# Rotary embedding on one core: one load merged, one store split in two, one small ScalarE copy moved back

## The chip, the cores and the metric

The kernel runs on 1 core of one Trainium2 chip. The metric is the time of one execution on the device in microseconds (us), so less is better. Before the change the median of 3 runs is 161.59 us; the three are 161.46, 161.59 and 163.9.

## The reference

The input `x` is 16 x 512 x 1024 float32 (33.55 MB), read as 16 heads of 64 numbers per token. Each head is cut into two halves of 32 and rotated by a table of cosines and sines that depends on the position alone:

```python
x = x.reshape(batch, seq, num_heads, head_dim)
x1, x2 = x[..., :half_dim], x[..., half_dim:]
rotated = np.concatenate([x1 * cos - x2 * sin,
                          x1 * sin + x2 * cos], axis=-1)
return rotated.astype(np.float32)
```

`cos` and `sin` are 512 x 32 float32. The output has the size of the input, so at least 67.1 MB cross between the chip's main memory (HBM) and the core's own memory.

## The kernel before

**Slabs and places.** `x` is cut into 8 slabs of 2 batches (4.19 MB each), which are worked on in pairs 0-1, 2-3, 4-5, 6-7. In a pair every one of the 128 partitions holds 16 successive tokens, 8 of the one slab and 8 of the other, so that a partition's 64 KB of a pair are contiguous in HBM, and one slab's share of it is 32 KB. There are three places in the core's memory, of a pair each. Slabs 0-5 fill them; slabs 6 and 7 are loaded into the places of slabs 0 and 1, once these have been stored.

**Transfers.** All loads of `x` are issued on SyncE's queue, all stores on ScalarE's, the two small tables ahead of everything on ScalarE's. Slabs 0, 1, 6 and 7 are loaded one by one (`load`, line 65, 128 rows of 32 KB each). Slabs 2-3 are loaded by two DMAs, one for even and one for odd partitions (line 83: 64 rows of 64 KB each). Slabs 4-5 are loaded by one DMA (128 rows of 64 KB). Slabs 0 to 3 are stored one by one (`store`, line 69); slabs 4-5 by two DMAs, of even and of odd partitions (line 162); slabs 6-7, the last, by one DMA of 128 rows of 64 KB (`store(6, 2)`).

**Table.** GpSimd makes a 0/1/-1 matrix (`pick`) and rounds cos and sin to bf16; TensorE spreads them by 8 small matmuls to the layout of the slabs, into two accumulators. The first half of the table (`tabs[0]`, for even slabs) is copied out by VectorE (line 113), the second (`tabs[1]`, for odd slabs) by ScalarE (line 144).

**Work on a slab.** ScalarE casts the slab to bf16 into the lower half of the place (`cast`); VectorE multiplies it twice with the table and adds the two with halves exchanged; ScalarE copies the sum back to float32 over the place, and the store is issued behind that copy. Slab 0 is worked in two passes, slab 7 in three. The copies of ScalarE stand in program order (`tc.keep_in_program_order`), and a cast runs ahead of the copies back by two slabs' places in the list: the cast of slab 2 stands in front of the copy back of slab 1, and so on. Line 138 in the profile is the helper `copy` by which all of ScalarE's copies go.

The order of ScalarE around the change is: cast slab 0 (two halves), copy `tabs[1]`, cast slab 1, copy back slab 0 (two halves), store 0, cast slab 2, copy back slab 1, store 1.

Of the kernel before, what the change touches and what calls it, by code (L numbers as in the profile page):

```python
# [2 lines left out]

# [4 lines left out]


@with_exitstack  # L10
def kernel(
    ctx: ExitStack,
    tc: tile.TileContext,
    x: bass.AP,
    cos: bass.AP,
    sin: bass.AP,
    num_heads: int,
    out: bass.AP,
):
    nc = tc.nc  # L20
    P = nc.NUM_PARTITIONS

    batch, seq, dim = x.shape
    nh = num_heads
    hd = dim // nh
    half = hd // 2
    bf16 = mybir.dt.bfloat16
    f32 = mybir.dt.float32

    nb = 2  # L30
    nslabs = batch // nb
    rpp = nb * seq // P
    W = rpp * dim
    TP = seq // rpp
    TW = rpp * half

    out_flat = out.rearrange("b s h d -> b s (h d)")

    singles = ctx.enter_context(tc.tile_pool(name="singles", bufs=1))
    pairs = ctx.enter_context(tc.tile_pool(name="pairs", bufs=3))  # L40
    psum = ctx.enter_context(tc.tile_pool(
        name="psum", bufs=1, space=bass.MemoryType.PSUM))


    def view(t, offset, *dims):
        return dataclasses.replace(t, offset=t.offset + offset,
                                   ap=[t.ap[0], *[list(d) for d in dims]])

    places = [pairs.tile([P, 2 * W], f32, tag="pair", name="pair") for _ in range(3)]


    def here(s, n=1):
        return view(places[s // 2 % 3], s % 2 * W, (1, n * W))


    def there(t, s, n=1):
        return bass.AP(tensor=t.tensor, offset=t.offset + s // 2 * 2 * P * W + s % 2 * W,  # L60
                       ap=[[2 * W, P], [1, n * W]])


    def load(s, n=1):
        nc.sync.dma_start(out=here(s, n), in_=there(x, s, n))  # L65


    def store(s, n=1):
        nc.scalar.dma_start(out=there(out_flat, s, n), in_=here(s, n))  # L69


    load(0)


    cos_sb = singles.tile([TP, TW], f32, tag="cos_sb")
    sin_sb = singles.tile([TP, TW], f32, tag="sin_sb")
    for t, src in ((cos_sb, cos), (sin_sb, sin)):
        nc.scalar.dma_start(out=t, in_=bass.AP(
            tensor=src.tensor, offset=src.offset, ap=[[TW, TP], [1, TW]]))

    load(1)
    for p in range(2):
        nc.sync.dma_start(out=here(2, 2)[p::2], in_=there(x, 2, 2)[p::2])  # L83
    load(4, 2)


    pick = singles.tile([TP, 4 * P], bf16, tag="pick")
    nc.gpsimd.memset(pick, 0.0)  # L88
    for h in range(2):
        for g in range(2):  # L90
            part = view(pick, (2 * h + g) * P, (TP // 2, 2 * P // TP), (1, TP // 2))
            nc.gpsimd.affine_select(  # L92
                out=part, in_=part, compare_op=mybir.AluOpType.not_equal,
                fill=1.0 - 2.0 * g, base=-h, pattern=[[0, 2 * P // TP], [-2, TP // 2]],
                channel_multiplier=1)

    tab1 = singles.tile([TP, 2 * TW], bf16, tag="tab1")
    for i, t in enumerate((cos_sb, sin_sb)):
        nc.gpsimd.tensor_copy(out=view(tab1, i * TW, (1, TW)), in_=t)  # L99

    accs, tabs = [], []
    for h in range(2):
        acc = psum.tile([P, 2 * rpp * hd], f32, tag=f"acc{h}", name="acc")
        for i in range(2):
            for f in range(2):
                nc.tensor.matmul(  # L106
                    view(acc, i * rpp * hd + f * half, (hd, rpp), (1, half)),
                    view(pick, (2 * h + i * f) * P, (1, P)),
                    view(tab1, i * TW, (half, rpp), (1, half)),
                    start=True, stop=True)  # L110
        accs.append(acc)
        tabs.append(singles.tile([P, 2 * rpp * hd], bf16, tag=f"tab{h}", name="tab"))
    nc.vector.tensor_copy(out=tabs[0], in_=accs[0])  # L113

    passes = []
    for s in range(nslabs):
        r = 0  # L120
        for n in {0: (4, 4), nslabs - 1: (4, 2, 2)}.get(s, (rpp,)):
            passes.append((s, r, n))
            r += n


    def halves(u):
        s, r, n = u
        t = here(s).bitcast(bf16)
        return [view(t, (2 * r + i * n) * dim, (1, n * dim)) for i in range(2)]


    def cast(u):
        s, r, n = u
        copy(halves(u)[0], view(here(s), r * dim, (1, n * dim)))


    def copy(out, in_):
        tc.keep_in_program_order(nc.scalar.copy(out=out, in_=in_))  # L138


    ahead = list(passes)
    for _ in range(2):
        cast(ahead.pop(0))
    copy(tabs[1], accs[1])
    cast(ahead.pop(0))
    for i, u in enumerate(passes):
        s, r, n = u
        while ahead and len(passes) - len(ahead) < (i + 2 if s < nslabs - 2 else len(passes)):
            cast(ahead.pop(0))
        lo, up = halves(u)  # L150
        for t, a in ((up, 0), (lo, rpp * hd)):
            nc.vector.tensor_mul(  # L152
                out=t, in0=lo,
                in1=view(tabs[s % 2], a + r * hd, (hd, n), (0, nh), (1, hd)))
        nc.vector.tensor_add(  # L155
            out=up, in0=up, in1=view(lo, half, (hd, n * nh), (-half, 2), (1, half)))

        copy(view(here(s), r * dim, (1, n * dim)), up)
        if r + n == rpp:
            if s == 5:  # L160
                for p in range(2):
                    nc.scalar.dma_start(out=there(out_flat, 4, 2)[p::2], in_=here(4, 2)[p::2])  # L162
            elif s == 7:
                store(6, 2)
            elif s < 4:
                store(s)
            if s < 2:
                load(s + 6)


# [1 line left out]
_INS = ['x', 'cos', 'sin', 'num_heads']  # L172
_OUTS = [((16, 512, 16, 64), 'float32')]

_NUMBERS = {'num_heads': 16}


# [26 lines left out]
```

## Time and profile before

| | |
|---|---|
| median of the runs | 161.59 us |
| time of the profiled execution | 161.8 us |
| its span, first to last instruction | 160.0 us |
| busy: VectorE, ScalarE | 107.9 us (67%), 114.3 us (71%) |
| busy: TensorE, GpSimd | 2.0 us, 2.6 us |
| HBM read, written | 33.69 MB, 33.55 MB |
| cast or copy back of a whole slab on ScalarE | 7.02 us |
| one of VectorE's three steps on a whole slab | 4.42 us |
| copy of half a table: VectorE, ScalarE | 1.23 us, 1.00 us |

The profile is of one execution. The span leaves out 1.8 us of the execution's time (161.8 - 160.0) at its start and end. "ACT" is ScalarE, "DVE" VectorE, "POOL" GpSimd, "SP" SyncE; a "q" behind an engine's name stands for its issuing of DMAs, which is not counted as busy time. A DMA's "landing" is the moment when its semaphore says that all of it has arrived. The core has 16 DMA engines, on which the DMAs of both queues run. A DMA's rows (here of 32 or 64 KB) are the packets that the profile counts; in tables by stretches of time the DMA share counts a packet with its whole time in the stretch in which it begins, so that a short stretch can show a share over 1, and the share times the length of the stretch is the time per engine of the packets that began in it.

### The profile page before, as it was taken

To read this page: it belongs to the slowest core of one execution; us is meant where nothing else is said; L and a number is where in the kernel's file an instruction comes from. 1 tells how busy PE (TensorE), PEld (TensorE's weight loads), DVE (VectorE), ACT (ScalarE), POOL (GpSimd) and SP (SyncE) were. 2 spreads that over 40 slices of the span, in tenths; PEclk is the share of its full clock that TensorE was granted. 3 is DMA by queue.
4 is the path that set the end of the run, shared out by engine and by line. 5 is a ranking of instruction groups with operands and counts; after the bars stand their busy time and mean duration, and the time that the engine had idled before them with its cause. 6 is when DMAs were issued, how large, how long until landed. Compare 5 with 4: busy or idle time off the path is not lost.

```text
span 160.0 us, 167 instructions
## 1 busy us (share of the span) xinstructions
PE 2.0 (1%) x8; PEld 1.0 (1%) x8; DVE 107.9 (67%) x34; ACT 114.3 (71%) x24; POOL 2.6 (2%) x11
## 2 busy tenths in 40 slices
PE   0001300000000000000000000000000000000000
PEld 0000100000000000000000000000000000000000
DVE  0000499999951999799889979998999998000000
ACT  3006959993089989998998999999879999500000
POOL 4000000000000000000000000000000000000000
DMA  7999999699599999999999999999997999989966
GB/s 262 401 401 410 426 491 524 262 524 524 254 401 410 606 426 393 393 393 393 467 451 393 434 483 393 401 500 410 393 590 328 524 393 393 524 360 426 524 262 262
DMA packets 1920, 67.24 MB, mean 420 GB/s; under 512 B 256, under 2 KB 384, under 8 KB 384
## 3 DMA queue, kind: packets, MB, share of 16 engines
q1 hardware_dynamic: 880, 33.55, 49.5%
q10 hardware_dynamic: 1040, 33.69, 48.7%
HBM read 33.69 MB, written 33.55 MB: 420 GB/s over the span
## 4 chain that ended last, share of the span: by engine, by line
ACT 52%; DMA 26%; issue 5%; ACTq 1%; SPq 1%; another core or an unknown queue 0%
ACT pair L138 52%; DMA pair<-in_x_dram 26%; ACTq L162 1%; ACTq L69 1%; SPq L65 0%; SPq L83 0%; ACTq L138 0%
## 5 line engine op out<-in xcount | busy, mean ns | idle before, releaser
L138 ACT CAST pair<-pair 128x8192 bf16<-128x8192 f32 (+5 forms) x22 | 112.1, 5155 | 21.9 <-DMA pair<-in_x_dram 19.8
L152 DVE TENSOR_TENSOR pair<-pair,tab 128x8192 bf16<-128x8192 bf16 (+2 forms) x22 | 71.4, 3259 | 9.3 <-ACT pair L138 8.9
L155 DVE TENSOR_TENSOR pair<-pair 128x8192 bf16<-128x8192 bf16 (+2 forms) x11 | 35.8, 3260 | 0.3
L113 DVE CAST tab<-acc 128x1024 bf16<-128x1024 f32 x1 | 1.2, 1225 | 18.3 <-PE acc L106 18.3
L138 ACT ACT_TABLE_LOAD x1 | 1.3, 1283 | 2.0 <-issue 2.0
L106 PE MATMUL acc<-tab,pick 64*128 64x256 bf16 x8 | 2.0, 403 | 17.1 <-POOL tab L99 17.1
L106 PEld LDWEIGHTS <-pick 64*128 64x128 bf16 x8 | 1.0, 127 | 17.6 <-issue 15.6
L92 POOL TENSOR_SCALAR_AFFINE_SELECT pick<-pick 64x128 bf16<-64x128 bf16 x4 | 1.1, 303 | 0.1
L138 ACT CAST tab<-acc 128x1024 bf16<-128x1024 f32 x1 | 1.0, 1004 | 0.0
L99 POOL CAST tab<-cos_sb 64x256 bf16<-64x256 f32 x1 | 0.4, 391 | 9.5 <-DMA cos_sb<-in_cos_dram 9.5
L88 POOL MEMSET pick<- 64x512 bf16 x1 | 0.5, 519 | 0.3 <-POOLq L185 0.3
L99 POOL CAST tab<-sin_sb 64x256 bf16<-64x256 f32 x1 | 0.4, 396 | 4.9 <-DMA sin_sb<-in_sin_dram 4.9
L185 POOL MEMSET const-float32-0.0<- 128x1 f32 x1 | 0.1, 104 | 0.2 <-issue 0.2
L185 POOL MEMSET const-bfloat16-1.0<- 128x1 bf16 x1 | 0.1, 107 | 0.0
L185 POOL MEMSET const-uint8-127<- 128x1 uint8 x1 | 0.1, 107 | 0.0
L185 POOL MEMSET const-float32-1.0<- 128x1 f32 x1 | 0.1, 104 | 0.0
## 6 DMA issues: line engine op xcount, KB each, us to landing
pair<-in_x_dram SPq DMA_DIRECT2D x4, 4096.0 KB, 22.5
out_dram<-pair ACTq DMA_DIRECT2D x4, 4096.0 KB, 32.8
cos_sb<-in_cos_dram ACTq DMA_DIRECT2D x1, 64.0 KB, 11.1
sin_sb<-in_sin_dram ACTq DMA_DIRECT2D x1, 64.0 KB, 15.8
pair<-in_x_dram SPq DMA_DIRECT2D x3, 42.2
out_dram<-pair ACTq DMA_DIRECT2D x3, 21.0
```

The source lines that it names most:

```text
L69: nc.scalar.dma_start(out=there(out_flat, s, n), in_=here(s, n))
L88: nc.gpsimd.memset(pick, 0.0)
L92: nc.gpsimd.affine_select(out=part, in_=part, compare_op=mybir.AluOpType.not_equal, fill=1.0 - 2.0 * g, base=-h, pattern=[[0, 2 * P // TP] ...
L99: nc.gpsimd.tensor_copy(out=view(tab1, i * TW, (1, TW)), in_=t)
L106: nc.tensor.matmul(view(acc, i * rpp * hd + f * half, (hd, rpp), (1, half)), view(pick, (2 * h + i * f) * P, (1, P)), view(tab1, i * TW, ( ...
L113: nc.vector.tensor_copy(out=tabs[0], in_=accs[0])
L138: tc.keep_in_program_order(nc.scalar.copy(out=out, in_=in_))
L152: nc.vector.tensor_mul(out=t, in0=lo, in1=view(tabs[s % 2], a + r * hd, (hd, n), (0, nh), (1, hd)))
L155: nc.vector.tensor_add(out=up, in0=up, in1=view(lo, half, (hd, n * nh), (-half, 2), (1, half)))
L162: nc.scalar.dma_start(out=there(out_flat, 4, 2)[p::2], in_=here(4, 2)[p::2])
L185: nc = _bacc.Bacc("TRN2", target_bir_lowering=False, num_devices=1)
```

## The change

Three edits, and no change of what is computed:

1. The two loads of slabs 2-3 (even, odd partitions) become one load of all 128 partitions.
2. ScalarE's copy of `tabs[1]` moves from in front of slab 1's cast to behind it.
3. The last store, of slabs 6-7, is issued as two DMAs, of even and odd partitions, by the same lines that do so for slabs 4-5.

```diff
@@ -79,8 +79,7 @@
     load(1)
-    for p in range(2):
-        nc.sync.dma_start(out=here(2, 2)[p::2], in_=there(x, 2, 2)[p::2])
+    load(2, 2)
     load(4, 2)
@@ -139,10 +138,9 @@
     ahead = list(passes)
-    for _ in range(2):
+    for _ in range(3):
         cast(ahead.pop(0))
     copy(tabs[1], accs[1])
-    cast(ahead.pop(0))
     for i, u in enumerate(passes):
@@ -157,13 +155,12 @@
         if r + n == rpp:
-            if s == 5:
+            if s < 4:
+                store(s)
+            elif s % 2:
                 for p in range(2):
-                    nc.scalar.dma_start(out=there(out_flat, 4, 2)[p::2], in_=here(4, 2)[p::2])
-            elif s == 7:
-                store(6, 2)
-            elif s < 4:
-                store(s)
+                    nc.scalar.dma_start(out=there(out_flat, s - 1, 2)[p::2],
+                                        in_=here(s - 1, 2)[p::2])
             if s < 2:
                 load(s + 6)
```

## The prediction, made before the changed kernel was run

> **What bounds the kernel now.** I read the DMA part of the page first, then busy times by stretches cut at the waves of packets, then ScalarE's timeline and the chain that ended last. The page's DMA queues (packets, MB, share of the 16 engines' span):
>
> ```profile
> q1 hardware_dynamic: 880, 33.55, 49.5%
> q10 hardware_dynamic: 1040, 33.69, 48.7%
> HBM read 33.69 MB, written 33.55 MB: 420 GB/s over the span
> ```
>
> Loads (q1) and stores (q10) together fill 98.2% of the span, 157.1 of 160.0 us. The rest is 2.9 us. The stretches show where it lies (start:end, length, busy us of PE, PEld, DVE, ACT, POOL, clock, DMA share, GB/s):
>
> ```profile
> 0.00:1.70 1.70, 0.00 (x0) 0.02 (x1) 0.00 (x0) 0.00 (x0) 1.10 (x7) 1.00 0.00 0
> 1.70:2.20 0.50, 0.00 (x0) 0.08 (x1) 0.00 (x0) 0.21 (x1) 0.50 (x3) 1.00 3.75 1049
> ...
> 36.80:37.30 0.50, 0.00 (x0) 0.00 (x0) 0.50 (x1) 0.47 (x1) 0.00 (x0) 1.00 4.84 2097
> 37.30:39.30 2.00, 0.00 (x0) 0.00 (x0) 1.97 (x2) 0.00 (x0) 0.00 (x0) 1.00 0.00 0
> 39.30:39.70 0.40, 0.00 (x0) 0.00 (x0) 0.40 (x1) 0.00 (x0) 0.00 (x0) 1.00 7.58 2621
> ...
> 72.50:138.90 66.40, 0.00 (x0) 0.00 (x0) 60.13 (x20) 63.35 (x14) 0.00 (x0) 1.00 1.00 434
> ```
>
> ```profile
> 126.90:127.50 0.60, 0.00 (x0) 0.00 (x0) 0.60 (x2) 0.60 (x1) 0.00 (x0) 1.00 4.03 1748
> 127.50:129.30 1.80, 0.00 (x0) 0.00 (x0) 1.80 (x3) 1.80 (x1) 0.00 (x0) 1.00 0.00 0
> 129.30:129.90 0.60, 0.00 (x0) 0.00 (x0) 0.60 (x1) 0.60 (x1) 0.00 (x0) 1.00 4.05 1748
> 136.60:137.20 0.60, 0.00 (x0) 0.00 (x0) 0.00 (x0) 0.60 (x1) 0.00 (x0) 1.00 3.78 1638
> 137.20:139.00 1.80, 0.00 (x0) 0.00 (x0) 0.00 (x0) 0.98 (x1) 0.00 (x0) 1.00 0.00 0
> 139.00:139.60 0.60, 0.00 (x0) 0.00 (x0) 0.00 (x0) 0.00 (x0) 0.00 (x0) 1.00 4.05 1748
> ...
> 156.00:156.50 0.50, 0.00 (x0) 0.00 (x0) 0.00 (x0) 0.00 (x0) 0.00 (x0) 1.00 4.84 2097
> ```
>
> A share of 4.84 over 0.50 us is 2.42 us per engine: one 64 KB row on each of the 16, begun together. Such a wave begins every 2.42 us: 36.8 and 39.3 in the loads, 126.9 and 129.3 in the store of slabs 4-5, 136.6 (its last), 139.0 (the first of slabs 6-7), 156.0 (the last of all, done at about 158.9). So the engines idle for 1.7 us at the start and about 1.1 at the end (158.9 to 160.0), and nowhere between: the kernel is bound by its transfers. ScalarE's timeline (start, us, what):
>
> ```profile
> 20.37 1.00 ACT L138 CAST tab<-acc 128x1024 bf16<-128x1024 f32 x1
> 23.24 14.04 ACT L138 CAST pair<-pair 128x8192 bf16<-128x8192 f32 x3 [1.87 <-DMA pair<-in_x_dram]
> 37.30 0.35 ACTq L69 DMA_DIRECT2D out_dram<-pair  x1
> 44.49 13.94 ACT L138 CAST pair<-pair 128x8192 bf16<-128x8192 f32 x2 [7.22 <-DMA pair<-in_x_dram]
> ...
> 73.41 13.94 ACT L138 CAST pair<-pair 128x8192 bf16<-128x8192 f32 x2 [0.62 <-DMA pair<-in_x_dram]
> ...
> 115.58 1.22 ACTq L162 DMA_DIRECT2D out_dram<-pair  x2
> 116.83 21.34 ACT L138 CAST pair<-pair 128x4096 bf16<-128x4096 f32 x7 [1.29 <-issue]
> 138.21 0.34 ACTq L69 DMA_DIRECT2D out_dram<-pair  x1
> ```
>
> The chain that ended last names ScalarE for 52%, from 44.49 on, where it waited for slabs 2-3, until it issues the last store at 138.21. But the first wave of that store begins at 139.0, just when the wave of 136.6 is through (136.6 + 2.42). ScalarE and the DMA engines arrive at the last store together. So neither a faster ScalarE nor an earlier landing helps alone, but whatever makes ScalarE later is paid in full.
>
> **The copy of `tabs[1]`.** It leaves the 1.87 us gap in front of slab 1's cast, where it is free, and stands behind that cast, at 30.26 (23.24 + 7.02). The copies back of slab 0 and the issue of store 0 move by its 1.00 us, the latter to 38.30. The next in line, slab 2's cast, waits for its load until 44.49 after an idle 7.22 us, which become 6.2: cost 0. Without that cover it would be 1.00. VectorE needs `tabs[1]` for slab 1 at 33.05; it is ready at 31.3 instead of 21.4, so 1.8 us are left. Store 0 enters the DMA engines 1 us later, while they have all of slabs 4-5 (8.4 MB) queued, so none idles. Today the wave begun at 39.3 takes 7.58 x 0.40 = 3.03 us instead of 2.42 as store 0 joins, and the first store rows begin after 42.2, before the load counts as landed at 44.44. If store 0 comes too late for that slot, the load lands when its wave ends, at about 42.2 to 42.5. So slabs 2-3 land 0 to 2.2 us earlier, and slabs 4-5 0 to 1.2 (a 32 KB row). I take 0, as the load must miss the slot on all 16 engines; and ScalarE's gain ends at the DMA engines anyway. Store 0 landed at 69.7 (37.30 + 32.4; the loading of slab 6 waits for it), and lands about 1 us later; slabs 4-5 still keep the load queue busy to 73.4. Slab 6 landed near 92.7 (69.8 + 22.9) for a cast at about 101.8 (87.77 and two steps of 7.02), slab 7 at 113.4 (90.4 + 23.0) for one at 116.83: 3.4 us of slack, of which 1 goes.
>
> **One load for slabs 2-3.** SyncE issues one DMA in about 0.59 us (the issue of slabs 4-5) instead of two in 1.24; the load of slabs 4-5, queued behind it, is issued 0.65 us sooner but begins only after 41.7. The rows are the same, 128 of 64 KB, 8 waves an engine, and the cast waited for both halves before. No row shows a 64 KB-row load of all partitions alone on the engines. Nearest are the two halves (36.80: 2.42 us a wave), and slabs 4-5 beside the stores, whose share of 1.00 leaves no more. Bounds: -0.6 us, if the slow wave goes, to +1.2, if a store row slips in ahead. I take 0.
>
> **Two DMAs for the last store.** Their rows are those of the store of slabs 4-5, which run at 2.42 us a wave, and across its two DMAs (126.9 to 129.3) without a gap. The issue takes 1.22 us (115.58) instead of 0.34. Only the first of the two, half of that, stands before the first wave, so the rows can come up to about 0.3 us later; the second has 4 waves, 9.7 us, to be issued in. It also waits for an older store's semaphore that it shares, which by the order of the queues is store 1's; that landed at 90.3 (58.47 + 31.8). Cost 0 to 0.3, and I take 0.1, as today's store shows no gap.
>
> A rule speaks against this edit. The Trainium skill, "DMA: Bandwidth & Descriptors" (Anatomy of one DMA — SWDGE (gpsimd) path), gives each DMA about 2 us of fixed cost, mostly completion, by a fit for DMAs that GpSimd issues, which these are not. An estimate by that page is +2.0 us on the tail, 163.6. The trace's row is the boundary inside slabs 4-5: 0 there.
>
> **Sum.** 0 + 0 + 0.1 on a span of 160.0 gives 160.1. The profiled execution's time was 161.8, the median 161.59. So 161.59 + 0.1 = 161.7 us.
>
> **Rivals.**
> *A late ScalarE (slower).* From 73.4 on ScalarE is busy but for issues, so a later landing of slabs 4-5, or of slabs 2-3 beyond 44.4, moves the last store one for one. The mechanism is a merged load that loads the engines unevenly, the fullest one running two 64 KB rows more: +4.84, so 166.5. It passes 2% (3.2 us) from the second such row. For it: the third run before, 163.9, is 2.4 us up, one such row's time, and there is no slack in the tie. Against it: the merged load has the shape of slabs 4-5, which goes at full share.
> *A fixed cost in the tail.* The last DMA's completion is not hidden by a next one: 0.3 us of landing lie behind the last wave today. Were the odd half to start one wave late, +2.4, hence 164.0. Against it are the waves of 126.9 and 129.3.
> *An earlier everything.* The slow wave at 39.3 becomes a normal one, -0.6, with ScalarE moving too: 161.0. For it: store 0 is issued 1 us later. To be faster by 2% the kernel would have to find 3.2 us, more than the whole 2.9 us in which the DMA engines idle.
> *The halves are no change.* If two half DMAs and one whole one are the same packets in the same order, edits 1 and 3 do nothing, and the time stays 161.6; it can't be told from the forecast.
>
> **How the numbers follow.** Forecast, with the last rival: 0.72. Late ScalarE 0.08, tail cost 0.09, earlier everything 0.09, faster by more than I can explain 0.02. About 2% is what a measurement of this kernel can tell from no change; below 158.4 is faster, above 164.8 slower. Faster 0.02. Slower is the late ScalarE and a little of the tail, 0.10. Same 0.88. The forecast by itself reaches from 161.0 (-0.6) to 163.1 (161.6 + 0.3 of issue + 1.2 of a slipped row). The range 160.9 to 163.1 is that, with the 0.1 by which the two lower runs differ below the earlier case; it leaves out late ScalarE, the tail and the 0.02: 0.19.
>
> **What would show it.** Right: DMA share 98% again; store 0 issued near 38.3; slab 2's cast between 42.3 and 44.5; the two last issues near 138.2 and 138.8; the last 8 waves 2.42 us apart with none missing at their middle. Wrong: a stretch of over 0.5 us without waves before 156; `tabs[1]` or slab 7 named as what an engine waited for; ScalarE's last issue after 138.6.

## The result, and the profile after

Over 22 executions each, run side by side, the changed kernel took 163.75 us in the median (161.66 to 165.36), the kernel before 161.75 (161.46 to 165.79). The ratio is 1.0067 with a 95% interval of 1.0041 to 1.0092; it leaves out executions more than 1.5% above the fastest of their kernel, and so a part of the difference. By the 2% that count as a difference the verdict is no change, but the kernel did get slower: it falls more often in the upper of two groups. Both kernels' executions divide so, with nothing between 162.3 and 163.0. The lower one is the same in both: medians of 161.74 before and 161.73 after. The upper one lies mostly from 163.6 to 165. Before, 4 of the 22 were above 163 us; after, 15 of 22.

The profiled execution after the change is one of the upper group (164.58 us, span 162.8). The page's DMA queues and the lines of the chain that ended last:

```profile
q1 hardware_dynamic: 864, 33.55, 48.6%
q10 hardware_dynamic: 1056, 33.69, 48.0%
HBM read 33.69 MB, written 33.55 MB: 413 GB/s over the span
...
DMA pair<-in_x_dram 42%; DMA out_dram<-pair 20%; ACT pair L137 19%; SPq L65 0%
```

The bytes are the same, but the engines are now occupied for 96.6% of a longer span (98.2% before), and ScalarE's share of the chain has fallen from 52% to 19%. In its place the chain goes through a store and a load. In order of time (start, us, what):

```profile
58.15 32.45 DMA out_dram<-pair
...
90.67 26.63 DMA pair<-in_x_dram
117.30 0.02 issue
117.32 13.37 ACT pair L137 x4
```

Store 1 lands at 90.6 and lets slab 7's load go; that load takes 26.6 us (23.0 before), lands at 117.3, and ScalarE has been waiting for it. Its issue has hardly moved (90.4 before). What has moved is slab 6's load, ahead of it in the same queue: that one landed at 92.7 before, and now at 97.9 (73.3 + 24.6). ScalarE's timeline:

```profile
30.42 1.01 ACT L137 CAST tab<-acc 128x1024 bf16<-128x1024 f32 x1
...
38.47 0.35 ACTq L69 DMA_DIRECT2D out_dram<-pair  x1
44.18 13.94 ACT L137 CAST pair<-pair 128x8192 bf16<-128x8192 f32 x2 [5.74 <-DMA pair<-in_x_dram]
...
117.32 21.23 ACT L137 CAST pair<-pair 128x4096 bf16<-128x4096 f32 x7 [2.02 <-DMA pair<-in_x_dram]
138.58 1.44 ACTq L162 DMA_DIRECT2D out_dram<-pair  x2
```

The copy of the table and store 0 stand close to where the prediction put them (30.42 for 30.26, 38.47 for 38.30). The last store is issued at 138.58 instead of 138.21. That is 0.4 us, and the span grew by 2.8. The rest shows in the busy times by stretches at the end (the next to last number is the DMA share):

```profile
139.60:140.00 0.40, 0.00 (x0) 0.00 (x0) 0.00 (x0) 0.00 (x0) 0.00 (x0) 1.00 6.17 2621
156.40:156.90 0.50, 0.00 (x0) 0.00 (x0) 0.00 (x0) 0.00 (x0) 0.00 (x0) 1.00 4.85 2097
156.90:159.00 2.10, 0.00 (x0) 0.00 (x0) 0.00 (x0) 0.00 (x0) 0.00 (x0) 1.00 0.00 0
159.00:163.00 4.00, 0.00 (x0) 0.00 (x0) 0.00 (x0) 0.00 (x0) 0.00 (x0) 1.00 0.04 16
```

The wave of 156.4 to 156.9 was the last of all before, 0.4 us earlier. Now something begins after 159.0: a share of 0.04 over 4.00 us is 0.16 us per engine on the average of 16, which is one row of 64 KB (2.42 / 16 = 0.15). The DMA queues from 158.5 to 163 have that row, beside 16 packets of under 512 bytes:

```profile
q10 hardware_dynamic: 17, 0.07, 3.6%
```

One DMA engine is a row behind the other 15, and they have nothing left to do while it finishes. That engine leaves the order of the others at store 0's first rows, in the DMA queues' answer for 41.7 to 43.2 us (packets, MB, share). Before, and after:

```profile
q10 hardware_dynamic: 16, 0.52, 80.9%
```

```profile
q10 hardware_dynamic: 15, 0.49, 75.8%
q1 hardware_dynamic: 2, 0.07, 10.1%
```

Before, all 16 engines turn to the first row of store 0 (q10) in this slot. After, 15 do, and the sixteenth begins a semaphore write and a 64 KB row of slabs 4-5 (q1: 0.07 MB) in its place. From there that engine's rows of store 0 come later than the others'. The missed slot by itself costs the engine no time, as it moves a load row in it. The trace does not name a packet's engine, but rows can be strung together, each beginning where the one before it ends. By that every engine moves 4.19 MB of loads and stores, and the one that missed the slot is the one that ends last. It alone has rows that begin after 42 us and take over 0.3 us longer than others of their size: 0.7 us longer at 46.6, 1.2 at 76.4 and 0.5 at 88.5. These 2.4 us are the row that it is behind at the end.

What the missed slot does change is the landing of store 0. Store 0 counts as landed when the last engine is done: at 73.2 (38.47 + 34.7) instead of 69.7. Only then is slab 6's load issued, at 73.3 instead of 69.8, when slabs 4-5 are in (ScalarE begins on them at 73.17). So the load queue is empty, where before slabs 4-5 had 3.6 us to go to their landing (73.4) when slab 6 was added. SyncE's timeline from 60 us on, before and after:

```profile
69.79 20.89 SPq L65 DMA_DIRECT2D pair<-in_x_dram  x2
```

```profile
73.29 17.71 SPq L65 DMA_DIRECT2D pair<-in_x_dram  x2
```

### The profile page after: what moved, and what is told of

It is laid out like the page before. It is cut to its first block, busy times and chain, and to the rows that moved or that the text cites. A ratio compares the mean times of both kernels' runs of the same rounds, so it can differ in the third digit from the quotient of the medians.

```text
span 162.8 us, 166 instructions
## 1 busy us (share of the span) xinstructions
PE 2.0 (1%) x8; PEld 1.0 (1%) x8; DVE 107.9 (66%) x34; ACT 114.2 (70%) x24; POOL 2.6 (2%) x11
## 4 chain that ended last, share of the span: by engine, by line
DMA 62%; ACT 19%; issue 3%; SPq 0%
DMA pair<-in_x_dram 42%; DMA out_dram<-pair 20%; ACT pair L137 19%; SPq L65 0%
```

## The experiments

The count of executions above 163 us tells more here than a median alone. For the kernel before it is 12 of 84 over all comparisons (4 of 22, 1 of 31, 3 of 17, 4 of 14).

| kernel | executions | above 163 us | median, us | ratio to before, 95% interval |
|---|---|---|---|---|
| copy moved alone | 8 | 7 | 164.44 | 1.0086, 1.0051 to 1.0120 |
| load merged alone | 12 | 2 | 161.81 | 1.0004, 0.9991 to 1.0017 |
| last store split alone | 11 | 1 | 161.92 | 1.0008, 1.0000 to 1.0017 |
| load and store, copy in its place | 11 | 1 | 161.88 | 1.0009, 1.0000 to 1.0018 |
| one further copy | 6 | 5 | 164.08 | none given |
| two further copies | 6 | 6 | 164.27 | 1.0158, 1.0124 to 1.0193 |
| three further copies | 6 | 6 | 164.25 | 1.0146, 1.0122 to 1.0171 |
| the change again | 12 | 8 | 163.97 | 1.0056, 1.0016 to 1.0097 |
| slab 6's load held back | 9 | 3 | 162.80 | 1.0081, 1.0035 to 1.0127 |

**Which edit.** Four kernels, each with a part of the change. The copy alone:

```diff
-    for _ in range(2):
+    for _ in range(3):
         cast(ahead.pop(0))
     copy(tabs[1], accs[1])
-    cast(ahead.pop(0))
```

> Only the copy of the table's second half moves behind slab 1's cast; loads and stores as before. Theory (moved copy: store 0 is issued 1 us later, one DMA engine then takes a 64 KB load row before its first store row, falls out of step, and store 0, slab 6, slab 7 and the last store follow late): two groups of executions as in the changed kernel, near 161.7 and near 163.7 to 165, the upper with about half of them or more; in a profile of the upper kind store 0 lands near 73 instead of 69.7. Rival 1 (merged load): all near 161.7 as before. Rival 2 (split last store): all near 161.7.

Seven of eight are above 163, the median is 164.44. The profile is of the upper kind, and again one engine takes a load row in store 0's first slot. The DMA queues from 41.7 to 43.2, then SyncE's timeline, then ScalarE's:

```profile
q10 hardware_dynamic: 15, 0.49, 75.9%
q1 hardware_dynamic: 2, 0.07, 12.6%
```

```profile
73.51 17.68 SPq L65 DMA_DIRECT2D pair<-in_x_dram  x2
```

```profile
38.57 0.35 ACTq L69 DMA_DIRECT2D out_dram<-pair  x1
...
117.61 21.23 ACT L138 CAST pair<-pair 128x4096 bf16<-128x4096 f32 x7 [2.24 <-DMA pair<-in_x_dram]
138.87 0.34 ACTq L69 DMA_DIRECT2D out_dram<-pair  x1
```

Slab 6's load goes out at 73.51, slab 7 is waited for, the last store leaves at 138.87. The moved copy makes the whole effect by itself. The load alone:

```diff
-    for p in range(2):
-        nc.sync.dma_start(out=here(2, 2)[p::2], in_=there(x, 2, 2)[p::2])
+    load(2, 2)
```

> Only the load of slabs 2-3 is one DMA. Theory (moved copy): as before the change, near 161.7 with the few higher executions that the kernel before also has (4 of 22 above 163). Rival 1 (the merged load puts an engine out of step): the upper group near 163.7 to 165 holds half or more.

Two of twelve, median 161.81: no effect. The last store alone:

```diff
-            if s == 5:
-                for p in range(2):
-                    nc.scalar.dma_start(out=there(out_flat, 4, 2)[p::2], in_=here(4, 2)[p::2])
-            elif s == 7:
-                store(6, 2)
-            elif s < 4:
+            if s < 4:
                 store(s)
+            elif s % 2:
+                for p in range(2):
+                    nc.scalar.dma_start(out=there(out_flat, s - 1, 2)[p::2],
+                                        in_=here(s - 1, 2)[p::2])
```

> Only the last store is two DMAs. Theory (moved copy): lower group 161.7 to 162.0, 0 to 0.3 us above before for the longer issue, upper group no larger than before (4 of 22). Rival 2 (the split store costs the time): all executions up by 2 us, near 163.7, or the upper group at half or more.

One of eleven, and the median is 0.14 us above before's 161.78. ScalarE's timeline shows the issue, 1.13 us in place of 0.34:

```profile
138.15 1.13 ACTq L164 DMA_DIRECT2D out_dram<-pair  x2
```

Both together, with the copy left where it was:

> The changed kernel with the table copy left in its place ahead of slab 1's cast: load merged, last store split. Theory (moved copy): back to the kernel before, median near 161.8, few executions above 163. If load or store matter, or only all three together, the upper group stays at half or more, median near 163.7.

One of eleven, 161.88. So the copy's place is the cause, and the other two edits don't add to it. In the profiles of these last three kernels all 16 engines take store 0's first row in its slot (16 packets of q10, 0.52 MB, from 41.7 to 43.2), and slab 6's load goes out at 69.6 to 69.7.

**The copy's place, or store 0's moment.** The kernel before, with its copy where it was, and the same copy done again n times (1, 2 or 3) behind slab 1's cast, so that store 0 is late while VectorE has its table early:

```diff
     copy(tabs[1], accs[1])
     cast(ahead.pop(0))
+    for _ in range(n):
+        copy(tabs[1], accs[1])
```

> The kernel before, with its table copy where it was, and the same copy of 1.0 us done a second time behind slab 1's cast: store 0 is issued near 38.4 as in the changed kernel, but VectorE has its table early. Theory (the moment at which store 0 reaches the DMA engines): two groups as with the moved copy, half or more of the executions above 163. Rival (it is the late table, or something else of the copy's place): as before, near 161.75 with about one in ten above 163.

Five of six above 163. Store 0 is issued at 38.50, and this time three engines fall out of step: from 41.7 to 43.2 the stores begin 13 rows, the loads three (0.20 MB) beside semaphore writes.

```profile
q10 hardware_dynamic: 13, 0.43, 65.7%
q1 hardware_dynamic: 7, 0.20, 32.0%
```

So it is the moment of store 0, not the table. With two and three further copies:

> The same with two further copies: store 0 near 39.4. Theory: still at the edge between two slots (load waves begin near 39.3 to 40.0 and the next 2.42 us later), so some engines take a load row first and others do not: the upper group holds half or more. Rival (a later store 0 simply costs its lateness): every execution about 1 us above those of one further copy.

> The same with three further copies: store 0 near 40.4, 3 us later than before. Theory: all 16 engines take a load row first, stay in step, slabs 2-3 land near 42.5, and the time is back at 161.6 to 161.9 with few executions above 163, although store 0 is later than in the slow kernels. Rival (lateness costs): median at 165 or more, worse than with one or two further copies.

All six executions of both are above 163. With two copies all 16 engines take a load row already (16 rows, 1.05 MB, from 41.7 to 43.2), where some were expected to and others not. With three they do as expected, but the time is not back at 161.6 to 161.9. Nor does store 0's lateness add up: the medians are 164.08, 164.27 and 164.25 for one, two and three copies. With three copies, the DMA queues from 41.7 to 43.2, SyncE's timeline, and ScalarE's:

```profile
q1 hardware_dynamic: 32, 1.05, 164.8%
```

```profile
72.05 17.46 SPq L65 DMA_DIRECT2D pair<-in_x_dram  x2
```

```profile
40.49 0.35 ACTq L69 DMA_DIRECT2D out_dram<-pair  x1
42.84 13.94 ACT L138 CAST pair<-pair 128x8192 bf16<-128x8192 f32 x2 [2.38 <-DMA pair<-in_x_dram]
...
118.21 21.23 ACT L138 CAST pair<-pair 128x4096 bf16<-128x4096 f32 x7 [4.27 <-DMA pair<-in_x_dram]
139.47 0.34 ACTq L69 DMA_DIRECT2D out_dram<-pair  x1
```

All 16 engines take a load row (1.05 MB) in this slot and stay in step, and slabs 2-3 reach ScalarE at 42.84, 1.7 us sooner than before. But store 0 now lands at 72.0, beside slabs 4-5 (71.8), so slab 6's load again meets an empty queue. By the trace's packets its rows then begin 5 us after the issue, and the rows around 76 and 86 us take 0.4 to 0.7 us longer on nearly all engines. Two engines lose more there, up to 2 us, and end last, at 160.5 and 161.3; the others end by 160.0. Slab 7 is late, and so is the last store. My theory of engines out of step was too narrow: a late store 0 costs also when they keep in step.

**The change again**, for a profile of the lower group:

> The changed kernel once more, beside the others on this chip. Theory: half or more of its executions above 163, the rest near 161.8; if a profile falls in the lower group, all its engines take the first row of store 0 in the same slot and store 0 lands before 70.5.

Eight of twelve above 163, and the profile fell in the lower group (161.83 us, span 160.0). The DMA queues from 41.7 to 43.2, SyncE's and ScalarE's timelines:

```profile
q10 hardware_dynamic: 16, 0.52, 81.0%
```

```profile
69.67 20.86 SPq L65 DMA_DIRECT2D pair<-in_x_dram  x2
```

```profile
38.47 0.35 ACTq L69 DMA_DIRECT2D out_dram<-pair  x1
...
138.17 1.13 ACTq L162 DMA_DIRECT2D out_dram<-pair  x2
```

Store 0 is issued at 38.47 as in the upper profile, to a hundredth. But all 16 engines take its first row in the slot, slab 6's load goes out at 69.67, and everything behind is as before the change. In these two profiles of the same program the difference begins with whether one engine misses a slot.

**How much the late load costs by itself.** The kernel before, with slab 6's load held back by a small DMA ahead of it on SyncE's queue (the diff leaves out a `return` that `load` got):

```diff
-            if s < 2:
-                load(s + 6)
+            if s == 2:
+                late = singles.tile([1, 16], f32, tag="late")
+                tc.keep_in_program_order(nc.sync.dma_start(out=late, in_=dataclasses.replace(
+                    here(2), ap=[[here(2).ap[0][0], 1], [1, 16]])))
+                tc.keep_in_program_order(load(6))
+                tc.keep_in_program_order(load(7))
```

> The kernel before with its store 0 on time, but slab 6's load held back: on SyncE's queue a DMA of 64 bytes stands in front of it that reads slab 2's result, so the load is issued near 73 instead of 69.8, when slabs 4-5 have just landed. Theory as it stands now (what costs is that the load queue runs dry because slab 6's load is issued after slabs 4-5 are through; its rows then join late, slab 7 comes too late for ScalarE, and the last store goes out late): nearly all executions above 163, slab 7's cast near 117.5 or later, no engine taking a load row before store 0's first row. Rival (the cost is engines out of step at store 0's first row, or store 0's lateness by itself): as before, near 161.75 with about one in ten above 163.

Six of nine lie between 162.70 and 162.92, one at 163.10, two above 164: slower than before by 1.0 us in the median. I had expected nearly all above 163. SyncE's timeline, ScalarE's, and the busy times by stretches at the end:

```profile
72.73 0.58 SPq L169 DMA_DIRECT2D late<-pair  x1
73.42 11.09 SPq L65 DMA_DIRECT2D pair<-in_x_dram  x2
```

```profile
118.08 21.23 ACT L138 CAST pair<-pair 128x4096 bf16<-128x4096 f32 x7 [2.65 <-DMA pair<-in_x_dram]
139.35 0.34 ACTq L69 DMA_DIRECT2D out_dram<-pair  x1
```

```profile
155.90:157.10 1.20, 0.00 (x0) 0.00 (x0) 0.00 (x0) 0.00 (x0) 0.00 (x0) 1.00 0.00 0
157.10:158.50 1.40, 0.00 (x0) 0.00 (x0) 0.00 (x0) 0.00 (x0) 0.00 (x0) 1.00 1.73 749
158.50:163.00 4.50, 0.00 (x0) 0.00 (x0) 0.00 (x0) 0.00 (x0) 0.00 (x0) 1.00 0.00 0
```

Slab 7 is late by the same road, the last store leaves 1.1 us later (139.35), and all 16 engines end together: 1.73 x 1.40 is the 2.42 us of one whole wave, with no row behind it. So the late load by itself costs about 1 us, through ScalarE, and does not make the upper group: three of nine above 163 are no clear excess over 4 of 14 beside them. In the profile after the change it costs 0.4 us (138.58 for 138.21), and the other 2.4 are the engine that ends a row behind. What makes rows take longer there, and not here, was not tried.

**A way out that told nothing.** In three kernels store 0 was issued as even and odd partitions from two queues, so that it would land before slabs 4-5 whatever its moment:

```diff
+        if s == 0:
+            for p, q in enumerate((nc.scalar, nc.gpsimd)):
+                q.dma_start(out=there(out_flat, 0)[p::2], in_=here(0)[p::2])
+            return
```

Made of the changed kernel, of three further copies, and of the kernel before:

> The changed kernel, with store 0 issued as two DMAs, even partitions from ScalarE's queue and odd ones from GpSimd's, so that two rings of store rows stand against the one of loads and store 0 lands some 10 us sooner. Theory (dry load queue): slab 6's load is issued before 65, the upper group is gone, time 161.6 to 162.4. Rival (store 0's late joining itself): half or more still above 163.

> The kernel with three further copies (store 0 near 40.4, all six executions above 163 so far), with store 0 over the same two queues. Theory: slab 6's load is issued before 68, and the time comes down to 161.6 to 162.4 although store 0 is as late as before. Rival (lateness of store 0 costs, by whatever way): stays near 164.

> The kernel before, with store 0 over the two queues. Theory: slab 6's load issued near 60 to 64, no execution above 163, median 161.5 to 162.0: no faster than before in its lower group, since the 16 DMA engines are busy throughout, but without the one in ten of its executions near 164. If a dry store queue behind the early store 0 costs as much as a dry load queue: 162.2 or more in all.

Medians of 193.87, 192.83 and 187.79 us. The waits of the first say why:

```profile
DVE pair L154 <- DMA out_dram<-pair: 33.5, 1, 33.5
```

VectorE's first step on slab 1 waits for the landing of store 0. In the trace VectorE waits ahead of that instruction for the same two semaphores as SyncE ahead of slab 6's load, those of store 0's halves; in the kernel before it has no such wait. It is likely, though not shown, that a store which steps over partitions of a place is taken by the framework to touch the neighbouring slab. The wait is the program's, so these runs say nothing on the theory.

## Why the prediction was right, and where it was wrong

**The ceiling held.** The transfers bound the kernel, no kernel here was faster, and the lower groups of all kernels without a late store 0 have medians between 161.66 and 161.92.

**The merged load at 0 was right:** 1.0004 with an interval across 1.

**The split last store at 0.1 us was right:** 0.14 in the medians. The fixed cost of about 2 us per DMA from the Trainium skill, "DMA: Bandwidth & Descriptors" (Anatomy of one DMA — SWDGE (gpsimd) path), does not show here, where the DMA stands queued behind another: the estimate from it, 163.6, lies above ten of eleven executions (161.75 to 162.05).

**The moved copy at 0 was wrong,** and with it the 161.7 for most executions. The ratio puts the time at 162.8 (161.75 x 1.0067), inside the range, but the median of all executions lies 0.65 us above its end. That the ratio lies inside is luck as far as the copy goes: the range reached to 163.1 for a longer issue and a slipped row of the merged load, and neither is what happened. The copy itself did cost ScalarE nothing, as was said. The step that failed is the one behind it: "Store 0 enters the DMA engines 1 us later, while they have all of slabs 4-5 (8.4 MB) queued, so none idles", with bounds of 0 to 2.2 us of gain, taken as 0 "as the load must miss the slot on all 16 engines". I asked when the load's landing would change, for which the last engine counts, and not when the store's would, for which the last engine counts as well. One engine that misses the slot is enough to bring store 0 from 69.7 to 73.2. "[It] lands about 1 us later; slabs 4-5 still keep the load queue busy to 73.4" had a slack of 3.6 us for it, and one turn of a load row and a store row is 2.42 + 1.21 = 3.63 us. The 2.4 us of the longer rows had no term in the sum. The prediction's signs of being wrong did show: ScalarE waited for slab 7 (2.02 us), and its last issue came after 138.6 (139.1).

**The late ScalarE rival** had the outcome right, one engine a row behind and a last store that leaves late. Its mechanism was wrong, a merged load that loads the engines unevenly: that load alone changed nothing. It got 0.08; the outcome came in two executions of three.

**What stays open.** The three longer rows of the engine that ends last lie near where rows of another DMA join in, but why that engine pays and the others don't was not tried by itself. With two and three further copies, where no engine is out of step at store 0's first row, engines end late too, so the missed slot is not the only way. Nor is it shown why an engine misses the slot in one execution and not in the next; that the kernel before has its 12 of 84 by the same road was not seen in a profile.

## What to carry to other kernels

When a moved step has DMA issues behind it, follow each to its landing and to what waits for that: cover by an idle engine does not cover the transfer. On saturated DMA engines slack is to be counted in whole rows, on the worst of the 16 engines, and a slack of one turn is none. Where a time has two groups, count the executions in each before believing one profile or one median.

## What the runs showed of the hardware that was not expected

A DMA issued while the engines are busy with the other queue begins its rows late. By the trace's packets store 0, issued at 37.30, began at 42.3, and slab 6's load, issued at 72.05 with three further copies, at 77.2, about 5 us each. The delay is not one figure: slab 6's load took 3.9 us before the change (69.79 to 73.7) and 6.2 when held back (73.42 to 79.6). On idle engines slab 0's load, issued at 0.74, began at 1.7.

Loads and stores then take turns by row, not by bytes. From 50 to 60 us in the kernel before each queue began 48 rows, the loads 3.15 MB and the stores 1.57. So beside 64 KB load rows the 4.19 MB of store 0 took 32.4 us, where the last 8.39 MB took 21.0 alone.

And one engine can come apart from the others by a whole row: in the profile after the change three rows of one engine, between 46 and 91 us, took 2.4 us longer together than others of their size, and this was not made up in the 70 us that followed.
